# Attention's values' products one step later, with a fourth buffer, and a tile's transposes 12 steps later

## The chip, the cores and the metric

The kernel runs on one core of a Trainium2 chip. The metric is device time in microseconds (us) of one execution. The core's engines each work through a queue of their own in order: TensorE (PE) multiplies matrices, VectorE (DVE) and GpSimd (POOL) work elementwise, ScalarE (ACT) evaluates functions and casts, SyncE (SP) issues transfers. They wait for each other through semaphores.

## What is computed

The reference is one layer of a hybrid model on 2048 tokens of width 1024: retention with 4 heads in both directions, attention with 8 query heads and 2 key/value heads over 2048 own and 256 context keys, a projection, and a feed-forward part.

```python
ret = _ret_out(_bidir_retention(rq_h, rk_h, rv_h, log_gamma, s_f, s_b), rg, ret_gn_g)
s = einsum('bqkgd,bskd->bkgqs', q, k).astype(f32) * ATT_SCALE
p = softmax(s, axis=-1)
att = einsum('bkgqs,bskd->bqkgd', p, v)
x = x + g1 * (concatenate([ret, att], -1) @ w_out)
h2 = _modulate(_rmsnorm(x, norm2_g), sh2, sc2)
x = x + g2 * (square(relu(h2 @ w_ff1)) @ w_ff2)
out = _rmsnorm(x, final_norm_g)
```

## The kernel before

The program has three stages: input projections (to about 640 us), attention with retention and the output projection woven through it (to about 1650 us), and the feed-forward part, which is two blocks of matmuls in Strassen form. The change lies in the second stage.

That stage is written as a table of events. `on(k, phase, fn)` puts a call into step k; the steps are run in order, and within a step the phases in this order: begin, scores, piece, maximum, early, exp, cast, low, chain, pe, values, late, dma. Each engine's queue is what these calls issue, in that order. There is no planner behind it.

Attention goes over 32 groups (16 tiles of 128 queries, from the last to the first, times 2 key/value heads). A group takes NK = 18 steps, one block of 128 keys each, and the next group follows without a gap. For key block i, counted from the group's own start k:

- step k + i: PE multiplies the scores into a psum buffer `st` (two matmuls, lines 205 and 206; two buffers), and a row-minimum product `mp` for the next groups (line 168 or 172; two buffers), which DVE reduces a step later (line 181).
- step k + i + 1: ACT takes the exponential into half of `p32` (line 211; three buffers of two blocks).
- for each pair j of blocks, step k + 2j + 3: ACT casts the pair to 16 bits, `phi` (line 215).
- step k + 2j + 4: the remainder `plo` = p - phi, either both halves on POOL (line 222; pairs 0, 2, 4, 6 and 7) or one half on DVE in this step and one in the next (line 224).
- step k + 2j + 6: PE multiplies plo and phi with the values (lines 238 and 239, 16 matmuls) into the accumulators `o0` and `o1`. In the step after a group's last pair, ACT evacuates them.

The pool `pp`, with three buffers to a name, holds `p32`, `phi` and `plo`.

Retention and the output projection go over the tiles in the same steps, one tile in RF = 35 steps. Both use psum banks 0 and 1 (`psX`), of which there is one each. For a tile whose output step is k = R0 + 43 + 35 n: retention's output and attention's output are transposed through bank 1 at k - 11 and k - 6 (line 1540), the products with w_out fill 16 of the steps k to k + 19 in bank 0 (lines 1555 to 1557, three matmuls each), the row is squared on ACT, its root is taken, POOL multiplies x by it at k + 24 (`norm`, line 1582), and PE transposes the new rows in two groups of four (`transpose_x`, line 1587) through bank 1. A step behind each group DVE multiplies by the scale (`modulate`, line 1592) and POOL adds the shift (line 1597); another step later SP stores the result (line 1600). The next tile but one uses bank 1 too: retention's heads stand at k + 32 to k + 35, and ACT copies them out at k + 36.

x stays in one of four buffers named `xr` from its fetch at k - 2 until the last transpose. The product of modulate lies in a buffer `u`, of which there are two; the squares of the next tile write their unused output to the same two.

For four tiles (those of t = 11 to 8) POOL and ACT also form sums of pairs of new rows for the feed-forward part (`h_pair`, lines 71, 72 and 1649), in 13 steps spread over 28, which start behind the stores. When attention is done, at step `done`, the first weights and products of the feed-forward part begin (`prelude`).

The two functions that set the steps, and the two that hold the buffers, are these.

Of the kernel before, what the change touches and what calls it, by code (L numbers as in the profile page):

```python
# [13 lines left out]
F16 = mybir.dt.float16  # L14
# [8 lines left out]
P = 128  # L23
# [6 lines left out]
NK = NT + NC  # L30
# [25 lines left out]
def layer_kernel(ctx: ExitStack, tc: tile.TileContext, a: dict, out: bass.AP):  # L56
# [87 lines left out]
    class Group:  # L144
# [66 lines left out]
            nc.scalar.activation(self.p[kt // 2][:, kt % 2], self.s.pop(kt), AF.Exp, scale=HD**-0.5)  # L211

        def cast(self, j):
            hi = self.hi[j] = pp.tile([P, 2, 512], F16, name="phi", tag="phi")
            nc.scalar.activation(hi, self.p[j], AF.Copy)  # L215

        def low(self, j, i=None):
            if i in (None, 0):
                self.lo[j] = pp.tile([P, 2, 512], F16, name="plo", tag="plo")
            lo, p, hi = self.lo[j], self.p[j], self.hi[j]  # L220
            if i is None:
                nc.gpsimd.tensor_tensor(lo, p, hi, op=ALU.subtract)  # L222
            else:
                nc.vector.tensor_tensor(lo[:, i], p[:, i], hi[:, i], op=ALU.subtract)  # L224
# [35 lines left out]
    groups = [Group(n, *o) for n, o in enumerate(order)]  # L260


    with ExitStack() as st, tc.manual_schedule():
# [332 lines left out]
        def post(s, col, kind, i, x):  # L596
# [69 lines left out]
            elif col == C_AQ:  # L666
# [22 lines left out]

                do(s + 5, "turned", high)  # L690
                do(s + 5, "vec", low)
                do(s + 6, "store", lambda: nc.sync.dma_start(aq_d[i], x["z"]))
            else:
# [47 lines left out]

                do(s + 4, "hi", high)
                do(s + 5, "low", low)
                do(s + 6, "turn", turn_k)
                do(s + 7, "vec", lambda: nc.vector.tensor_copy(ks[:, :, row * P : (row + 1) * P], x["pt"][:, :2]))

        def value_parts(s):
# [50 lines left out]
            for i in range(3):  # L798
                do(s + 7 + i, "aux", scaled, i)
                do(s + 8 + i, "hi", high, i)  # L800
                do(s + 9 + i, "low", low, i)
# [274 lines left out]
        def slots(*what):  # L1076
            return [first[g, col] + n for g, col, ns in what for n in ns]

        two = (0, 0, 1, 1, 2, 2, 3, 3, 4, 4, 5, 5)
        at = slots((0, C_RQ, range(4)), (0, C_RV, two), (1, C_AQ, (1, 2, 3, 4)), (1, C_RK, (0, 0, 1, 2, 2, 3, 4, 4, 5)))  # L1080
# [6 lines left out]
        at = slots((0, C_AKV, range(1, 6)), (0, C_AQ, range(4)), (0, C_RQ, range(4)), (1, C_AQ, range(6)))  # L1087
# [12 lines left out]
        for i in range(NK):  # L1100
            at = min(s + i + 1, len(units) - 1)
# [128 lines left out]
    def pool(stack, name, bufs=1, **kw):  # L1230
        return stack.enter_context(tc.tile_pool(name=name, bufs=bufs, reuse_waits="tile", **kw))
# [4 lines left out]
    pp = pool(attn, "pp", 3)  # L1236
# [32 lines left out]
    def on(k, phase, fn, *args):  # L1269
        events.setdefault((k, phase), []).append((fn, args))  # L1270
# [25 lines left out]
    LAG = 22  # L1296
    ats = {}

    def attention():
        for n, g in enumerate(groups):  # L1300
            k = NK * n
            if n > 0:
                on(k - 14, "dma", g.load)
                on(k - 1, "late", g.minima, sm)
                for i in range(NK):
                    on(k + i, "piece", g.piece, i)
                    on(k + i + 1, "maximum", g.maximum, i)
            else:
                on(k + NK, "begin", g.load)
            on(k + NK, "chain", g.least, mts[n % 2])  # L1310
            on(k + NK + 1, "piece", g.turn)
            on(k + NK + 2, "cast", g.rows)
            on(k + NK + 3, "early", g.rows2)
            k += LAG
            for i in range(NK):
                on(k + i, "scores", g.scores, i)
                on(k + i + 1, "exp", g.exp, i)
            for j in range(NK // 2):
                on(k + 2 * j + 3, "cast", g.cast, j)
                if j in POOL_PAIRS:  # L1320
                    on(k + 2 * j + 4, "low", g.low, j)
                else:
                    for i in range(2):
                        on(k + 2 * j + 4 + i, "low", g.low, j, i)
                on(k + 2 * j + 6, "values", g.values, j)
            k += NK + 5
            on(k, "cast", g.evacuate)
            on(k + 1, "chain", g.invert)
            on(k + 2, "late", g.combine, ats)
        return NK * len(groups) + LAG + 8  # L1330

# [195 lines left out]
    def output_tile(t, k, last):  # L1529
# [94 lines left out]
                rest.extend([(f, q) for f in (transpose_x, modulate, shift_, store_h)])  # L1624
            return made, made + 5
        for q in range(2):
            at = k + (31 if t == 1 else 27) + q
            on(at, "pe", transpose_x, q)
            on(at + 1, "early", modulate, q)
            on(at + 1, "late", shift_, q)  # L1630
            on(at + 2, "dma", store_h, q)
# [39 lines left out]
    for i in range(3):  # L1671
        on(18 + i, "begin", more_keys, 0, i)
        on(26 + 4 * i, "late", more_keys, 1, i)
    done = attention()
    retention(24)
    output_weights(44)
    for n, t in enumerate(range(NT - 1, -1, -1)):
        made_at, last = output_tile(t, R0 + 43 + RF * n, n == NT - 1)
        if t in halves[0][4:]:
            for i, step in enumerate(h_pair(0, 11 - t)):  # L1680
                on(last + (2 + i if i < 2 else 4 + 2 * i), "dma" if i < 2 else "late", step)
# [424 lines left out]
    with tc.manual_schedule():  # L2106
# [8 lines left out]
        k = min(events)[0]  # L2115
# [67 lines left out]
```

## Time and profile before

| | us |
|---|---|
| median of 3 runs | 2825.27 (2821.01 to 2826.14) |
| profiled execution | 2820.49 |
| its span | 2818.7 |
| PE busy in the span | 2666.1 (95%) |
| DVE busy | 2180.7 (77%) |
| POOL busy | 1931.8 (69%) |
| ACT busy | 1467.6 (52%) |
| mean granted PE clock | 0.988 |

The profiled execution is the source of every duration below; it lies within the runs' spread. In the views, a row names the source line, the engine and the operation as out<-in, and a wait is written as "who <- for whom". [...] PEld is the loading of weights, which goes on beside the matmuls.

### The profile page before, as it was taken

How to read it: one execution, taken by the hardware profiler on the slowest of the kernel's cores; microseconds unless marked ns; L12 is line 12 of the kernel's file. 1: busy time of each engine (PE TensorE's matmuls, PEld its weight loads, DVE VectorE, ACT ScalarE, POOL GpSimd, SP SyncE). 2: the span in 40 equal slices, each digit the busy share in tenths (PEclk: the TensorE clock that was granted, in tenths of full speed). 3: DMA queues.
4: the chain of work that ended last, by engine and by line, in shares of the span. 5: the costliest groups of instructions: out<-in, count | busy, mean ns of one | idle time of the engine just before them, and what ended most of it. 6: DMA issues, size and time to landing. Idle time of an engine off the chain costs nothing.

```text
span 2818.7 us, 46098 instructions
## 1 busy us (share of the span) xinstructions
PE 2666.1 (95%) x16756; PEld 1600.5 (57%) x16756; DVE 2180.7 (77%) x3122; ACT 1467.6 (52%) x2443; POOL 1931.8 (69%) x1499
## 2 busy tenths in 40 slices
PE   6999999997899998999999889999999999999997
PEld 3878788875566665665666544444444444444443
DVE  3678748858987777787777469888876688888898
ACT  2534444425777777777777645555554322222232
POOL 2627428316865668787666679888775688888887
PEclk9999999999999999999999999999999999999998
DMA  6776956827312123333212454777783757575543
GB/s 213 271 258 212 325 216 204 270 100 236 114 43 75 52 66 101 117 93 95 63 61 73 172 163 132 230 249 244 244 275 106 254 180 283 173 275 172 188 142 112
DMA packets 330466, 482.81 MB, mean 171 GB/s; under 512 B 82807, under 2 KB 193655, under 8 KB 325758
## 3 DMA queue, kind: packets, MB, share of 16 engines
q1 hardware_dynamic: 329854, 479.60, 52.0%
q8 instruction: 132, 2.16, 0.3%
q14 instruction: 96, 0.79, 0.1%
q10 hardware_dynamic: 384, 0.26, 0.0%
HBM read 327.57 MB, written 152.20 MB: 170 GB/s over the span
## 4 chain that ended last, share of the span: by engine, by line
PE 57%; DVE 8%; POOL 5%; issue 3%; DMA 2%; ACT 1%; SPq 0%; POOLq 0%; DVEq 0%; ACTq 0%
PE pu L1789 7%; PE pu L1790 7%; PE pu L1791 7%; PE pd L2008 5%; PE pd L2007 5%; PE pd L2006 5%; PE o L239 3%; PE st L205 3%; PE st L206 3%; PE mp L168 2%; DVE nm L181 2%; PE bank L1555 2%; PE bank L1557 2%; PE bank L1556 2%; PE o L238 2%
## 5 line engine op out<-in xcount | busy, mean ns | idle before, releaser
L181 DVE TENSOR_REDUCE nm<-mp 128x1 f32<-128x512 f32 (+1 forms) x576 | 390.7, 684 | 172.3 <-PE mp L168 143.4
L222 POOL TENSOR_TENSOR plo<-p,phi 128x1024 f16<-128x1024 f32 x160 | 353.6, 2211 | 162.6 <-ACT phi L215 130.5
L211 ACT ACTIVATE p<-st 128x512 f32<-128x512 f32 x576 | 338.5, 598 | 197.7 <-PE st L206 122.4
L1789 PE MATMUL pu<-hf,w1f 128*128 128x512 f16 x896 | 340.9, 380 | 0.0
L2008 PE MATMUL pd<-w,uf 128*128 128x512 f16 x896 | 339.6, 379 | 1.3 <-DVE uf L1999 1.2
L1790 PE MATMUL pu<-hf,w1f 128*128 128x512 f16 x896 | 340.7, 380 | 0.0
L1791 PE MATMUL pu<-hf,w1f 128*128 128x512 f16 x896 | 340.6, 380 | 0.0
L2006 PE MATMUL pd<-w,uf 128*128 128x512 f16 x896 | 339.6, 379 | 0.0
L2007 PE MATMUL pd<-w,uf 128*128 128x512 f16 x896 | 339.6, 379 | 0.0
L215 ACT ACTIVATE phi<-p 128x1024 f16<-128x1024 f32 x288 | 303.9, 1055 | 0.0
L1020 PE MATMUL pso<-whi,hlo_l 128*128 128x512 f32 (+1 forms) x768 | 288.4, 376 | 10.6 <-DVE hlo_l L488 10.5
L1018 PE MATMUL pso<-whi,hhi_l 128*128 128x512 f32 (+1 forms) x768 | 296.9, 387 | 0.0
L1019 PE MATMUL pso<-wlo,hhi_l 128*128 128x512 f32 (+1 forms) x768 | 287.1, 374 | 1.7 <-DVE wlo L512 1.7
L238 PE MATMUL o<-wv,plo 128*128 128x65 f16 x2304 | 235.6, 193 | 25.2 <-POOL plo L222 18.1
L224 DVE TENSOR_TENSOR plo<-p,phi 128x512 f16<-128x512 f32 x256 | 240.9, 942 | 16.5 <-ACT phi L215 15.9
L2046 POOL TENSOR_TENSOR d<-d,g2b 128x512 f32<-128x512 f32 x126 | 200.9, 1595 | 69.5 <-DVE d L2018 67.7
L239 PE MATMUL o<-wv,phi 128*128 128x129 f16 x2304 | 243.4, 221 | 0.0
L238 PEld LDWEIGHTS <-plo 128*128 128x128 f16 x2304 | 206.3, 98 | 61.6 <-POOL plo L222 28.2
L1801 DVE TENSOR_TENSOR r<-pu,r 128x512 f32<-128x512 f32 x224 | 151.0, 686 | 111.2 <-PE pu L1791 92.2
L1806 POOL TENSOR_TENSOR r<-r 128x512 f32<-128x512 f32 x128 | 169.0, 1326 | 93.7 <-ACT r L1805 93.3
L205 PE MATMUL st<-qr,ks 128*128 128x512 f16 x576 | 219.6, 381 | 9.8 <-ACT p L211 9.7
L168 PE MATMUL mp<-ks,qr 128*128 128x512 f16 x512 | 196.3, 383 | 30.7 <-DVE nm L181 23.8
(324 smaller groups left out, 6306.3 us busy)
## 6 DMA issues: line engine op xcount, KB each, us to landing
wm<-in_w_ff SPq DMA_DIRECT2D x64, 512.0 KB, 6.7
u<-r SPq DMA_DIRECT2D x128, 256.0 KB, 4.8
ur<-u SPq DMA_DIRECT2D x128, 256.0 KB, 5.7
y<-x SPq DMA_DIRECT2D x64, 512.0 KB, 6.4
wst<-in_w_in SPq DMA_DIRECT2D x60, 512.0 KB, 6.6
wf<-w2f SPq DMA_DIRECT2D x112, 256.0 KB, 3.6
w<-wf SPq DMA_DIRECT2D x28, 1024.0 KB, 10.7
w1r<-in_w_ff SPq DMA_DIRECT2D x48, 512.0 KB, 5.7
```

Source lines behind the costliest of these rows:

```text
L181: nc.vector.tensor_reduce(dst, src, axis=AX.X, op=ALU.max, negate=True)
L205: mm(ps, ks[:, self.g, k], q[:, 0], start=True, stop=False)
L211: nc.scalar.activation(self.p[kt // 2][:, kt % 2], self.s.pop(kt), AF.Exp, scale=HD**-0.5)
L222: nc.gpsimd.tensor_tensor(lo, p, hi, op=ALU.subtract)
L238: mm(o[:, : HD + 1], lo[:, i, c], v[:, : HD + 1], start=False, stop=False)
L239: mm(o, hi[:, i, c], v[:, :VW], start=False, stop=last)
L1789: mm(pu[hf, i], whi, hi, start=k == 0, stop=False)
L1790: mm(pu[hf, i], whi, lo, start=False, stop=False)
L1791: mm(pu[hf, i], wlo, hi, start=False, stop=k == 3)
L2006: mm(ps, u[:, 0, b], w[:, b, 0], start=b == 0, stop=False)
L2007: mm(ps, u[:, 0, b], w[:, b, 1], start=False, stop=False)
L2008: mm(ps, u[:, 1, b], w[:, b, 0], start=False, stop=b == 3)
```

## The change

Four things are changed. The values' products of pair j are issued at k + 2j + 7, and a group's evacuation, its reciprocal and its combination also one step later; `attention` returns an end one step later, which moves the prelude. `phi` and `plo` have four buffers rather than three. The transposes of a tile's new rows stand at k + 39 and k + 41 rather than k + 27 and k + 28, with modulate, shift, store and, for the four tiles that have it, the pairs' work that follows. The tiles t = 1 (k + 31 and k + 32) and t = 0 (behind the loop) keep their places.

```diff
         def cast(self, j):
-            hi = self.hi[j] = pp.tile([P, 2, 512], F16, name="phi", tag="phi")
+            hi = self.hi[j] = pp.tile([P, 2, 512], F16, name="phi", tag="phi", bufs=4)
             nc.scalar.activation(hi, self.p[j], AF.Copy)

         def low(self, j, i=None):
             if i in (None, 0):
-                self.lo[j] = pp.tile([P, 2, 512], F16, name="plo", tag="plo")
+                self.lo[j] = pp.tile([P, 2, 512], F16, name="plo", tag="plo", bufs=4)
...
-                on(k + 2 * j + 6, "values", g.values, j)
-            k += NK + 5
+                on(k + 2 * j + 7, "values", g.values, j)
+            k += NK + 6
             on(k, "cast", g.evacuate)
             on(k + 1, "chain", g.invert)
             on(k + 2, "late", g.combine, ats)
-        return NK * len(groups) + LAG + 8
+        return NK * len(groups) + LAG + 9
...
         for q in range(2):
-            at = k + (31 if t == 1 else 27) + q
+            at = k + (31 + q if t == 1 else 39 + 2 * q)
             on(at, "pe", transpose_x, q)
             on(at + 1, "early", modulate, q)
             on(at + 1, "late", shift_, q)
             on(at + 2, "dma", store_h, q)
```

On PE, before, at the step in which retention's scores (L1394) of a tile begin, in the middle of the stage (st are scores, mp the row-minimum product, xr the normalized rows of the tile before, o the accumulators):

```order
L239 MATMUL o_11573<-wv,phi 128x129
L205 LDWEIGHTS ks
L205 MATMUL st<-qr,ks 128x512
L206 LDWEIGHTS ks_6522
L206 MATMUL st<-qr,ks_6522 128x512
L168 LDWEIGHTS qr
L168 MATMUL mp<-ks,qr 128x512
L1394 MATMUL bank_11926<-oqt,okt 128x128 x4
L1587 MATMUL bank_11931<-ident,xr 128x128 x4
L205 LDWEIGHTS ks
L205 MATMUL st<-qr,ks 128x512
```

On PE, after, at the same place:

```order
L205 LDWEIGHTS ks
L205 MATMUL st<-qr,ks 128x512
L206 LDWEIGHTS ks_6522
L206 MATMUL st<-qr,ks_6522 128x512
L168 LDWEIGHTS qr
L168 MATMUL mp<-ks,qr 128x512
L1394 MATMUL bank_11910<-oqt,okt 128x128 x4
L238 LDWEIGHTS plo
L238 MATMUL o_11588<-wv,plo 128x65
```

The values' products, which stood ahead of this step's scores, now stand behind the step's other work, and the transposes of xr are gone from here.

On PE, after, the place in the next tile to which the first of these transposes has come (mt are the row minima that are turned):

```order
L1557 MATMUL bank_12105<-wo,rl 128x512
L205 LDWEIGHTS ks
L205 MATMUL st<-qr,ks 128x512
L206 LDWEIGHTS ks_6522
L206 MATMUL st<-qr,ks_6522 128x512
L192 MATMUL mp<-ident,mt_6530 128x128 x4
L168 LDWEIGHTS qr
L168 MATMUL mp<-ks,qr 128x512
L1587 MATMUL bank_12216<-ident,xr 128x128 x4
L238 LDWEIGHTS plo
```

They stand among the next tile's output products (L1557 in the step before), again ahead of the values of their step.

On SP the stores of a tile's new rows (h<-u) stood together, after that tile's of load and ahead of the fetch of the next x. Now, for one tile (ogate is retention's gate, oqt, okt, ork and orv the next loads):

```order
L1356 DMA of<-sf_179 128x512
L1534 DMA xr<-in_x 128x1024
L157 DMA qr<-aq_128 64x4x128
L158 DMA qr<-aq_128 64x2x128
L157 DMA qr<-aq_128 64x4x128
L158 DMA qr<-aq_128 64x2x128
L1600 DMA h_201<-u 128x512
L1356 DMA ogate<-rg_114 128x512
L1600 DMA h_201<-u 128x512
L1356 DMA oqt<-qt_145 128x512
```

The two stores stand behind the next x and a group's four qr loads, with the gate's load between them.

## The prediction

> **What bounds the kernel now.** I read the page first: the engines' busy time, and the chain that ended last.
>
> ```profile
> span 2818.7 us, 46098 instructions
> PE 2666.1 (95%) x16756; PEld 1600.5 (57%) x16756; DVE 2180.7 (77%) x3122; ACT 1467.6 (52%) x2443; POOL 1931.8 (69%) x1499
> PE 57%; DVE 8%; POOL 5%; issue 3%; DMA 2%; ACT 1%; SPq 0%; POOLq 0%; DVEq 0%; ACTq 0%
> ```
>
> TensorE (PE) is busy for 95% of the span and leads the chain, so only time in which PE stands still can be won. The change touches the attention stage, so the table of windows comes next (us, busy time and instruction count of PE, PEld, DVE, ACT and POOL, then granted clock, DMA share, GB/s).
>
> ```profile
> 640.00:745.00 105.00, 87.18 (x842) 63.47 (x841) 96.32 (x188) 71.86 (x113) 79.45 (x55) 1.00 0.70 217
> 745.00:1060.00 315.00, 293.77 (x2757) 192.57 (x2755) 252.65 (x436) 240.82 (x393) 207.16 (x151) 0.99 0.19 56
> 1060.00:1300.00 240.00, 218.50 (x1990) 142.17 (x1988) 184.29 (x310) 182.36 (x304) 197.42 (x150) 0.98 0.38 106
> 1300.00:1610.00 310.00, 295.26 (x2740) 193.34 (x2738) 227.89 (x403) 230.87 (x380) 199.21 (x153) 1.00 0.26 86
> ```
>
> From 640 to 745 DVE is busy 96.32 of 105 us: that stretch is DVE's, and I count no gain in it. From 745 to 1610 PE is busy 807.5 of 865 us, so 57 us are idle. Who PE waits for there is the third view (total us, times, longest):
>
> ```profile
> PE o L238 <- POOL plo L222: 17.2, 14, 2.5
> PE mp L168 <- DVE nm L181: 9.4, 21, 1.4
> PE st L205 <- ACT p L211: 8.3, 12, 1.9
> PE bank L1587 <- POOL xr L1582: 6.7, 9, 1.5
> PE bank L1540 <- DVE u L1592: 5.2, 10, 1.3
> PE o L238 <- DVE plo L224: 5.1, 10, 1.0
> PE bank L1587 <- DVE u L1592: 0.5, 2, 0.4
> ```
>
> Line 238 is the values' product, lines 1587 and 1540 are transposes through the one psum bank 1. These five of the seven rows are what the change touches; the rows of mp and st are what it can make worse. The last view is the work of one step, as groups of this same window (busy us, mean ns):
>
> ```profile
> L205 PE MATMUL st<-qr,ks 128*128 128x512 f16 x515 | 196.0, 381 | 8.4 <-ACT p L211 8.3
> L211 ACT ACTIVATE p<-st 128x512 f32<-128x512 f32 x517 | 304.1, 598 | 169.0 <-PE st L206 107.1 <-POOL plo L222 35.1 <-DVE plo L224 20.6
> L215 ACT ACTIVATE phi<-p 128x1024 f16<-128x1024 f32 x259 | 273.3, 1055 | 0.0
> L222 POOL TENSOR_TENSOR plo<-p,phi 128x1024 f16<-128x1024 f32 x144 | 316.1, 2196 | 150.6 <-ACT phi L215 122.1 <-issue 16.2 <-DVE xr L1562 7.8
> ```
>
> 515 scores in 865 us make 1.68 us per step, 3.36 us per pair of steps. How the pieces lie in time is seen in one pair without output products in its second step (start, us, engine):
>
> ```profile
> 1086.50 0.60 ACT L211 ACTIVATE p<-st 128x512 f32<-128x512 f32 x1 [0.76 <-PE st L206]
> 1087.00 1.05 ACT L215 ACTIVATE phi<-p 128x1024 f16<-128x1024 f32 x1
> 1087.11 0.19 PE L238 MATMUL o<-wv,plo 128*128 128x65 f16 x1
> 1087.81 0.38 PE L205 MATMUL st<-qr,ks 128*128 128x512 f16 x1
> 1088.02 0.38 PE L206 MATMUL st<-qr,ks 128*128 128x512 f16 x1
> 1088.44 0.60 ACT L211 ACTIVATE p<-st 128x512 f32<-128x512 f32 x1 [0.39 <-PE st L206]
> 1088.93 0.87 ACT L1432 ACTIVATE oo<-oo,mr,cy_gn 128x128 f32<-128x128 f32 x2
> 1089.80 0.38 PE L205 MATMUL st<-qr,ks 128*128 128x512 f16 x1
> ```
>
> Three things are read here. A 512-column matmul is 0.38 us long, but the next starts 0.21 us behind it, so each row of idle time above hides some 0.16 us per stall. The values' products of one pair take 0.70 us of PE (1087.11 to 1087.81). And the casts (L215) stand between the exponentials of the even and of the odd step.
>
> **The change part by part, and its price.**
>
> *Values one step later.* No product is added. The products of a pair now stand behind the next step's scores and row-minimum product (three matmuls, 0.65 us) and whatever else PE has in that step; on average that is half of 3.36 less 0.70, or 1.33 us. So a wait on plo shrinks by 0.65 to 1.33 us; I take 1.0. POOL's 14 waits are 17.2/14 + 0.16 = 1.39 us each; some are shorter than 1.0, so I take 12 of their 19.4 us. DVE's ten are 5.1/10 + 0.16 = 0.67 us each and go whole: 6.7 us.
>
> *The fourth buffers.* L215, which fills phi, has 0.0 us idle before it, and POOL's L222 waits for phi's content (122.1 us), not for a place: buffers held nobody up, and the fourth is worth nothing by itself. It only keeps it so when a buffer is held a step longer. Bounds 0 and 1 us; I take 0.
>
> *Transposes 12 (and 13) steps later.* They wait for POOL's norm (L1582), whose result then lies 15 steps back, not 3; the bank is free after ocopy three steps ahead of them; the two groups stand two steps apart, so the second no longer follows on DVE's modulate, and neither do the transposes of L1540. Idle removed at most: 6.7 + 5.2 + 0.5 and 21 times 0.16, 15.8 us. But POOL is full where the largest of them lie:
>
> ```profile
> 1115.56 1.28 POOL L1388 TENSOR_TENSOR oqb<-oqt,tb 128x512 f32<-128x512 f32 x1
> 1116.80 1.16 POOL L72 TENSOR_TENSOR hp<-hs,hp 128x512 f16<-128x512 f32 x1
> 1117.95 1.12 POOL L1582 TENSOR_SCALAR xr<-xr,cy_f 128x1024 f32<-128x1024 f32 x1
> 1119.04 2.13 POOL L222 TENSOR_TENSOR plo<-p,phi 128x1024 f16<-128x1024 f32 x1
> 1122.57 2.48 POOL L1597 TENSOR_TENSOR u<-u,s 128x512 f32<-128x512 f32 x2
> 1119.12 0.66 PE L1587 MATMUL bank<-ident,xr 128*128 128x128 f32 x4 [1.05 <-POOL xr L1582]
> ```
>
> If L1587 no longer waits until 1119, the values that follow still wait for the plo that ends at 1121.17: PE merely gets there earlier. I take 60% of the 15.8, 9.5 us; the bounds are 5 (only the L1540 part) and 15.8.
>
> What else moves with them: modulate on DVE, shift (2.48 us for two) on POOL, two stores per tile on SP. The stores now stand behind the fetch of the next x and a group's four qr loads, and the gate's load behind the first of them. SP waits there for the shift; the gate is needed eight steps (13 us) later, so it is covered; without that cover each late load would cost POOL up to its landing time. The buffers of u are shared with the squares, whose next turn comes five steps (8 us) after the store is issued, against this landing time (last column, us):
>
> ```profile
> h<-u SPq DMA_DIRECT2D x32, 256.0 KB, 2.0
> ```
>
> Price 0, bounds 0 and 3 us. x stays 12 steps longer in its buffer, 43 of a 35-step period, so two of four buffers live: 0. The four tiles that also form h pairs do this 13 steps later, over the same lump of POOL work in the next tile: 0, bounds -4 and +4 us.
>
> *The clock.* Stalls in a row also cost clock:
>
> ```profile
> 1177.00:1180.30 3.30, 1.42 (x11) 0.99 (x10) 1.49 (x3) 0.34 (x1) 3.30 (x3) 1.00 0.71 141
> 1180.40:1187.00 6.60, 5.64 (x32) 3.98 (x33) 3.52 (x7) 3.21 (x5) 6.20 (x5) 0.50 0.27 76
> ```
>
> After a stretch with PE busy for 1.42 of 3.30 us, the clock is 0.50 for 6.6 us, which costs 3.3 us. I take 2.5 us back, bounds 0 and 5. [...]
>
> *What gets worse.* With the values moved, an odd step's scores follow the even step's 0.70 us sooner, while ACT is still in the cast. In the pair shown, the odd exponential would start when the cast ends, 1088.05, and end at 1088.65; the scores that need its buffer start at 1089.80 - 0.70 = 1089.10. The room falls from 0.76 to 0.45 us. ACT's other work between 745 and 1610 is 654.1 busy less 304.1 and 273.3, 76.7 us, about 118 lumps of 0.65 us; each that falls there overdraws 0.2 us. The output products, heads and scores of retention fill 21 of 35 steps and give room; in the other 40%, 47 lumps by 0.2 are 9.4 us. The minima (L168) lose the same 0.70 us against DVE: the room is wider, I take 2 us, bounds 0 and 5.
>
> *The end.* Everything after attention comes one step later, so one up-projection part (three matmuls) fewer stands ahead of this stall:
>
> ```profile
> 1619.87 0.66 PE L1587 MATMUL bank<-ident,xr 128*128 128x128 f32 x4 [4.45 <-POOL xr L1582]
> ```
>
> Its cover shrinks by 3 times 0.216: +0.65 us.
>
> Sum: -12 - 6.7 - 9.5 - 2.5 + 9.4 + 2 + 0.65 = -18.65 us. The profiled execution took 2820.49 us, 4.8 below the median of 2825.27; 2820.5 - 18.65 = 2801.8, and beside the median 2806.6. I forecast 2807 us.
>
> **Rivals.**
>
> *All of it comes out.* ACT's lumps fall where products give room, the transposes' waits do not return: -12 - 6.7 - 15.8 - 2.5 + 0.65 = -36 us, 2789 us. For it: outside 1060 to 1300 POOL is busy for only 207.16 of 315 us. Against it: the room of 0.45 us.
>
> *POOL keeps its lumps.* PE arrives earlier and waits for the same low parts: the 12 us of POOL's plo and 6.7 of the transposes' gain come back, -18.65 + 18.7 = 0, 2825 us. For it: between 1060 and 1300 POOL is busy 197.42 of 240 us. Against it: half of the waits lie elsewhere.
>
> *Slower: ACT becomes late for the odd scores.* ACT's exponential waits 35.1 + 20.6 = 55.7 us, in 39 stalls of 1.43 us, until a low part frees a p32 buffer, of which three are left as they are. With 0.45 us of room each such stall could reach PE as 0.98 us: 39 x 0.98 = 38 us, -18.65 + 38 = +19, 2844 us. It decides once exponentials end later than 0.45 us after where the shown pair has them, in most pairs. Against it: PE paid only 8.3 us on st so far.
>
> **How the numbers follow.** The sum's own case, 2796 to 2818 by its terms' bounds: 0.52. All comes out: 0.20. POOL keeps its lumps: 0.12. ACT late: 0.16. A difference under 0.2% (5.6 us) cannot be told from none in this kernel. Faster is 0.52 + 0.20 = 0.72, the same 0.12, slower 0.16. The range 2780 to 2830 holds the first three and the mild part of the last.
>
> **What the profile after would show.** Waits of L238 on plo at some 8 us rather than 22; L1587 and L1540 waits on xr and u nearly gone between 745 and 1610; L205 on ACT's p risen from 8 to some 17 us; fewer windows at half clock. I am wrong if the rows of st or mp grow by more than those of plo and the transposes shrink.

## The result, and the profile after

The changed kernel took 2824.40 us (median of 12 runs, 2821.59 to 2829.39), the kernel before 2822.74 us in the same comparison: a ratio of 1.0009, 95% interval 1.0002 to 1.0016. So nothing was won; by the interval 0.6 to 4.5 us were lost. Forecast were 2807 us. The profiled execution of before, 2820.49 us, lies below the three runs that were given with it (from 2821.01 us) and within the twelve of this comparison (2817.19 to 2826.49 us).

The page of the changed kernel's profiled execution:

```profile
span 2822.9 us, 46094 instructions
PE 2664.2 (94%) x16756; PEld 1604.0 (57%) x16756; DVE 2193.4 (78%) x3122; ACT 1457.6 (52%) x2443; POOL 1928.3 (68%) x1499
```

Who PE waits for between 745 and 1610 us, after (the view that the prediction shows of before):

```profile
PE st L205 <- ACT p L211: 16.4, 23, 2.5
PE mp L168 <- DVE nm L181: 15.1, 27, 1.8
PE o L238 <- POOL plo L222: 10.8, 8, 2.3
PE mp L192 <- DVE mt L187: 6.6, 6, 1.7
PE mp L172 <- DVE nm L181: 3.5, 6, 1.1
```

The transposes' rows (L1587, and L1540 on u) are gone, the values' wait on DVE is gone, that on POOL is down from 17.2 to 10.8 us. St is up from 8.3 to 16.4, and what ends in mp (L168, L172, and L192, the turning of the minima) is up from 11.9 to 25.2 us. For plo, the transposes and st that is near the forecast; for mp it is not. But this window does not cut the two programs at the same places: of the first five groups it holds 51.9 us before and 62.4 us after. From the first scores of the sixth group to the last scores of all, PE's waits are these. Before:

```profile
PE o L238 <- POOL plo L222: 16.9, 13, 2.5
PE bank L1587 <- POOL xr L1582: 6.7, 9, 1.5
PE mp L168 <- DVE nm L181: 6.1, 16, 1.0
PE bank L1540 <- DVE u L1592: 5.2, 10, 1.3
PE o L238 <- DVE plo L224: 4.3, 9, 1.0
PE st L205 <- ACT p L211: 2.7, 7, 0.6
PE mp L192 <- DVE mt L187: 1.2, 2, 0.7
...
```

After:

```profile
PE o L238 <- POOL plo L222: 10.8, 8, 2.3
PE mp L168 <- DVE nm L181: 10.2, 20, 1.2
PE st L205 <- ACT p L211: 7.3, 17, 0.9
PE mp L192 <- DVE mt L187: 6.6, 6, 1.7
PE mp L172 <- DVE nm L181: 2.2, 4, 1.1
```

Waits on plo fall by 10.4 us, and those of the transposes are gone (12.4 us, with a row of 0.5 that is not shown). St rises by 4.6 us, and mp by 11.2, from 7.8 (L172 has 0.5 of it) to 19.0. So there is a gain in this stretch. It is lost at both its ends, which is seen when the stage is cut at the same places of the program: first scores, first scores of the sixth group, last scores, first transposes of tile t = 1. Before:

```profile
638.50:796.90 158.40, 129.83 (x1233) 91.62 (x1232) 144.62 (x260) 112.28 (x178) 120.33 (x79) 0.98 0.51 157
796.90:1589.30 792.40, 746.53 (x6954) 488.95 (x6953) 606.40 (x1058) 602.82 (x989) 549.64 (x414) 0.99 0.26 76
1589.30:1619.90 30.60, 24.15 (x166) 13.45 (x162) 14.40 (x25) 13.11 (x25) 15.18 (x17) 1.00 0.89 346
```

After:

```profile
643.60:807.40 163.80, 131.27 (x1231) 93.51 (x1232) 147.81 (x259) 111.33 (x178) 117.96 (x79) 0.96 0.49 152
807.40:1583.90 776.50, 737.90 (x6935) 486.92 (x6932) 616.53 (x1056) 593.41 (x988) 547.42 (x412) 1.00 0.27 78
1583.90:1623.60 39.70, 25.20 (x182) 14.72 (x181) 16.27 (x27) 13.82 (x26) 18.11 (x19) 0.89 0.64 245
```

The first five groups take 5.4 us more, the stretch behind them 15.9 us less, the tail 9.1 us more: -1.4 us in all. From there to the end of the span it is 1198.8 and 1199.4 us. The 5.1 us by which the first scores start later (643.6 against 638.5) come from ahead of any changed instruction; they are this execution's, and the medians differ by 1.7 us only.

### The profile page after: what moved, and what is told of

Read it like the earlier page. It is cut to its first block, busy times and chain, and to the rows that moved or that the text cites. A ratio compares the mean times of both kernels' runs of the same rounds, so it can differ in the third digit from the quotient of the medians.

```text
span 2822.9 us, 46094 instructions
## 1 busy us (share of the span) xinstructions
PE 2664.2 (94%) x16756; PEld 1604.0 (57%) x16756; DVE 2193.4 (78%) x3122; ACT 1457.6 (52%) x2443; POOL 1928.3 (68%) x1499
## 3 DMA queue, kind: packets, MB, share of 16 engines
q1 hardware_dynamic: 329854, 479.60, 51.9%
## 4 chain that ended last, share of the span: by engine, by line
PE 57%; DVE 9%; POOL 3%; issue 2%; DMA 2%; ACT 2%; SPq 0%; POOLq 0%; DVEq 0%; ACTq 0%
PE pu L1789 7%; PE pu L1790 7%; PE pu L1791 7%; PE pd L2006 5%; PE pd L2007 5%; PE pd L2008 5%; PE o L239 3%; DVE plo L224 3%; PE st L205 3%; PE st L206 3%; PE mp L168 3%; DVE nm L181 2%; PE bank L1555 2%; PE bank L1557 2%; PE bank L1556 2%
## 5 line engine op out<-in xcount | busy, mean ns | idle before, releaser
L224 DVE TENSOR_TENSOR plo<-p,phi 128x512 f16<-128x512 f32 x256 | 256.4, 1003 | 18.5 <-ACT phi L215 13.4
L238 PE MATMUL o<-wv,plo 128*128 128x65 f16 x2304 | 232.9, 193 | 10.8 <-POOL plo L222 10.8
L168 PE MATMUL mp<-ks,qr 128*128 128x512 f16 x512 | 196.6, 384 | 35.8 <-DVE nm L181 28.5
```

The source lines that it names most:

```text
L238: mm(o[:, : HD + 1], lo[:, i, c], v[:, : HD + 1], start=False, stop=False)
```

## The experiments

Measured first, so that the verdicts can be read against it. "First five", "rest" and "tail" are the first three stretches above, from one profiled execution each; a ratio is to the kernel before on the same chip, with its 95% interval.

| kernel | median us | ratio | first five | rest | tail |
|---|---|---|---|---|---|
| before | 2822.2 to 2822.7 | 1 | 158.4 | 792.4 | 30.6 |
| changed | 2824.40 | 1.0009 (1.0002 to 1.0016) | 163.8 | 776.4 | 39.7 |
| values alone | 2825.19 | 1.0011 (1.0002 to 1.0020) | 164.4 | 789.3 | 30.1 |
| transposes alone | 2822.21 | 0.9998 (0.9989 to 1.0007) | 157.3 | 784.5 | 38.0 |
| all but tile 2 | 2816.09 | 0.9981 (0.9972 to 0.9991) | 165.5 | 779.1 | 30.2 |
| tile 2 alone | 2832.05 | 1.0027 (1.0017 to 1.0037) | 160.4 | 792.4 | 38.3 |
| values two later | 2816.75 | 0.9974 (0.9965 to 0.9984) | 159.5 | 780.4 | 32.4 |
| three buffers | 2821.09 | 0.9991 (0.9980 to 1.0001) | 165.2 | 776.9 | 39.7 |
| four p32 | 2819.20 | 0.9987 (0.9975 to 0.9998) | 163.2 | 783.6 | 30.5 |
| values from group 6 | 2812.84 | 0.9962 (0.9948 to 0.9977) | 158.7 | 781.6 | 30.4 |
| two later, four p32 | 2811.76 | 0.9965 (0.9952 to 0.9978) | 161.5 | 776.3 | 31.2 |
| transposes but tile 2 | 2817.48 | 0.9978 (0.9967 to 0.9989) | 161.0 | 789.3 | 29.7 |
| POOL's low later | 2810.11 | 0.9960 (0.9947 to 0.9974) | 160.3 | 778.7 | 30.7 |
| DVE's low later | 2817.63 | 0.9983 (0.9973 to 0.9992) | 163.5 | 781.4 | 30.7 |

Kernels that have the same program up to the sixth group (before, tile 2 alone, values from group 6, and the two with transposes alone) differ by up to 3.7 us in "first five": that is the spread of one execution. In "rest" the two kernels with transposes alone, which differ in tile 2's only, are 4.8 us apart, so differences of a few us there are not safe either.

### Which part, and which place

Values alone, against the kernel before:

```diff
-tag="phi")
+tag="phi", bufs=4)
-tag="plo")
+tag="plo", bufs=4)
-on(k + 2 * j + 6, "values", g.values, j)
-k += NK + 5
+on(k + 2 * j + 7, "values", g.values, j)
+k += NK + 6
-return NK * len(groups) + LAG + 8
+return NK * len(groups) + LAG + 9
```

> The values' products one step later with the four buffers; the transposes stay where they stood before. Measure for the tail: from the last scores to the first transposes of tile t = 1, 30.6 us before and 39.7 us in the changed kernel. Theory A (the tail's loss comes from tile t = 2's second store, behind which SP's seven loads of hf now stand): the tail is within 2 us of 30.6, attention keeps about half of its gain of 10 us, 2818 us against 2823. Rival B (the tail's loss comes from the prelude, one step later): the tail is 39 us here too, 2827 us. Rival C (the values' later place gives nothing, since st and mp wait for as much as plo no longer does): tail 30.6, attention as before, 2823 us.

Transposes alone:

```diff
-at = k + (31 if t == 1 else 27) + q
+at = k + (31 + q if t == 1 else 39 + 2 * q)
```

> The transposes 12 and 13 steps later; values, buffers and prelude as before. Theory A: the tail is 39 us, attention gains 6 to 9 us by the transposes alone, about 2823 us. Rival B: the tail is 30.6 us and the time 2815 us. Rival C: attention gains all its 10 us here, and with A's tail 2821 us.

The whole change without tile t = 2's transposes, against the changed kernel:

```diff
-at = k + (31 + q if t == 1 else 39 + 2 * q)
+at = k + ({1: 31, 2: 27}[t] + q if t in (1, 2) else 39 + 2 * q)
```

> The whole change, but tile t = 2's transposes stay at k + 27 and k + 28. Theory A: the loads of hf are issued some 8 us sooner than in the changed kernel, the tail is back at about 31 us, 2816 us, 8 under the changed kernel. Rival B: the tail stays at 39 us, 2824 us, as the changed kernel.

Tile t = 2 alone, against the kernel before:

```diff
-at = k + (31 if t == 1 else 27) + q
+at = k + (39 + 2 * q if t == 2 else (31 if t == 1 else 27) + q)
```

> The kernel before with one edit: tile t = 2's transposes at k + 39 and k + 41. Theory A: nothing but the tail changes, which becomes 38 to 40 us; 2831 us, 8 over before. Rival B: 2823 us, as before.

Three of the four came out as theory A has it, to within 1.1 us. The tail's loss follows the place of tile 2's transposes and not the prelude's: 38.0 and 38.3 us with them moved and the prelude at its old step, 30.1 and 30.2 us with the prelude a step later and them at their old place. Undoing this one place is worth 8 us (2816.09 against 2824.40), doing it alone costs 9 (2832.05; 5 to 10 by the ratio's interval).

How it costs them is seen on SP's queue. Before:

```profile
1585.53 1.77 SPq L1600 DMA_DIRECT2D h<-u  x2
...
1589.72 11.13 SPq L1779 DMA_DIRECT2D hf<-hf  x7
...
1608.36 1.49 SPq L1572 DMA_DIRECT2D x<-xr  x1
```

After:

```profile
1593.52 0.34 SPq L1600 DMA_DIRECT2D h<-u  x1
...
1597.04 0.32 SPq L1600 DMA_DIRECT2D h<-u  x1
1597.45 3.73 SPq L1779 DMA_DIRECT2D hf<-hf  x7
...
1605.32 8.76 SPq L1572 DMA_DIRECT2D x<-xr  x1
```

The seven loads of hf, 1 MB each, and the weights behind them keep the transfers busy in the tail (a DMA share of 0.89 and 346 GB/s in before's row of it). After, they stand behind tile 2's second store, and SP waits there for POOL's shift of those rows, which ends at 1597.01, until 1597.04. The loads that were issued from 1589.72 on, while attention still ran, are issued from 1597.45 on, although attention ends 5 us sooner. Tile 1's x is stored behind them (it lands 10.1 us after its issue before, 16.8 after), and POOL's norm, which overwrites x, waits for that store, 8.47 and 14.04 us. POOL's norm of tile 1, before and after:

```profile
1618.69 1.12 POOL L1582 TENSOR_SCALAR xr<-xr,cy_f 128x1024 f32<-128x1024 f32 x1 [8.47 <-DMA x<-xr]
```

```profile
1622.41 1.12 POOL L1582 TENSOR_SCALAR xr<-xr,cy_f 128x1024 f32<-128x1024 f32 x1 [14.04 <-DMA x<-xr]
```

and without tile 2's move:

```profile
1614.42 1.12 POOL L1582 TENSOR_SCALAR xr<-xr,cy_f 128x1024 f32<-128x1024 f32 x1 [7.03 <-DMA x<-xr]
```

Counted from the last scores, the norm starts after 29.4, 38.5 and 29.0 us. Tile 1's transposes wait for it, and PE with them: for 4.45 us before (the row that the prediction shows for the end), and after:

```profile
1623.58 1.12 PE L1587 MATMUL bank<-ident,xr 128*128 128x128 f32 x4 [12.25 <-POOL xr L1582]
```

Values alone is the miss: 2825.19 us where 2818 were expected. The tail is as A has it, but the first five groups lose 6 us, and the rest gains 3.1. There the plo waits did go, and others took their place:

```profile
PE st L205 <- ACT p L211: 14.9, 17, 2.5
PE bank L1587 <- POOL xr L1582: 14.3, 10, 3.1
PE mp L168 <- DVE nm L181: 13.8, 23, 1.8
...
PE o L238 <- POOL plo L222: 3.2, 1, 3.2
```

PE, no longer stopped by plo, reaches the transposes sooner and waits there for POOL's norm, 14.3 us rather than 6.7. With the transposes alone it is the other way round:

```profile
PE o L238 <- POOL plo L222: 24.5, 22, 3.0
PE mp L168 <- DVE nm L181: 13.1, 20, 2.0
PE st L205 <- ACT p L211: 6.5, 11, 1.5
```

plo's wait grew from 17.2 to 24.5 us. Each half hands part of its gain to the other's wait, since both end on POOL; together they win 16 us in the rest, singly 3.1 and 7.9. The waits show it more firmly than these three differences of single executions do.

### One step, two steps, and buffers

Values two steps later, tile 2 as before, against the changed kernel:

```diff
-on(k + 2 * j + 7, "values", g.values, j)
-k += NK + 6
+on(k + 2 * j + 8, "values", g.values, j)
+k += NK + 7
-return NK * len(groups) + LAG + 9
+return NK * len(groups) + LAG + 10
-at = k + (31 + q if t == 1 else 39 + 2 * q)
+at = k + ({1: 31, 2: 27}[t] + q if t in (1, 2) else 39 + 2 * q)
```

> As the run that keeps tile t = 2's transposes (2816.1 us), but the values two steps later than before, so that they stand in even steps again, with all the room that a step of either kind gives. Theory D (one step is harmful by its parity: the odd scores follow too soon on ACT and DVE): the first five groups take 158 us again rather than 165, PE waits for st 8 us and for plo under 3 us between 745 and 1610, 2806 us. Rival E (it is the lateness of the values itself, not the parity): the first five groups stay at 164 us, PE waits for st stay at 14 us, and only the plo waits fall: 2812 us.

The first five groups are back (159.5 us), so their loss belongs to the odd step, not to lateness. But st did not fall to 8 us. It rose:

```profile
PE st L205 <- ACT p L211: 31.2, 27, 3.5
```

while ACT waits for low parts to free p32:

```profile
ACT p L211 <- DVE plo L224: 38.1, 18, 4.6
ACT p L211 <- POOL plo L222: 22.5, 15, 3.7
```

When the values no longer stop PE for a late low part, the scores do, one buffer further on. Both theories named only a part of it: 2816.75 us, where they had 2806 and 2812.

Three buffers for phi and plo, against the changed kernel: the two `bufs=4` are taken out.

> The changed kernel with three buffers for phi and plo, as before the change. If the fourth buffer is worth nothing, 2824 us, within 2 us of the changed kernel. If buffers held one step longer hold up casts or low parts, PE waits for plo and st grow and the time is above 2830 us.

2821.09 us, 3.3 under the changed kernel, where 2 at most were expected; the ratios' intervals (0.9980 to 1.0001, and 1.0002 to 1.0016) just miss each other. So the fourth buffers win nothing here. Why the kernel without them should be 3 us below the changed one stays open: its profiled execution, itself one of 2825.44 us, shows nearly the same three stretches.

The fourth buffer for p32 (phi and plo three, tile 2 as before), against the changed kernel:

```diff
-name="p32", tag="p32")
+name="p32", tag="p32", bufs=4)
-tag="phi", bufs=4)
+tag="phi")
-tag="plo", bufs=4)
+tag="plo")
-at = k + (31 + q if t == 1 else 39 + 2 * q)
+at = k + ({1: 31, 2: 27}[t] + q if t in (1, 2) else 39 + 2 * q)
```

> As the run that keeps tile t = 2's transposes (2816.1 us), but the fourth buffer goes to p32, and phi and plo have three. Theory F (the scores' waits come from exponentials that wait for a low part to free p32): ACT's waits on plo fall from 56 us to under 20, PE's wait for st from 14.6 to about 6 us, 2808 us. Rival (they come from the cast that stands ahead of the odd exponential): PE's wait for st stays at 12 to 15 us, 2816 us.

ACT's waits for low parts nearly vanish (POOL's are 3.4 us, DVE's are not among the longest), but st only falls to 10.8 us and mp and plo rise:

```profile
PE mp L168 <- DVE nm L181: 19.2, 30, 1.8
PE o L238 <- POOL plo L222: 11.8, 7, 3.2
PE st L205 <- ACT p L211: 10.8, 10, 2.5
```

The time (2819.20 us) does not fall: with the values one step later p32's buffers are not what binds. Both, two steps and four p32 buffers, against the kernel before:

```diff
-name="p32", tag="p32")
+name="p32", tag="p32", bufs=4)
-on(k + 2 * j + 6, "values", g.values, j)
-k += NK + 5
+on(k + 2 * j + 8, "values", g.values, j)
+k += NK + 7
-return NK * len(groups) + LAG + 8
+return NK * len(groups) + LAG + 10
-at = k + (31 if t == 1 else 27) + q
+at = k + ({1: 31, 2: 27}[t] + q if t in (1, 2) else 39 + 2 * q)
```

> Values two steps later, four buffers for p32, three for phi and plo, the transposes 12 and 13 steps later but for tile t = 2. With the values out of the way PE waited 31 us for st, behind exponentials that waited for p32. If p32's buffers are what bound there: PE's wait for st falls to some 12 us, the stretch from the sixth group to the last scores is 770 us rather than 780, 2807 us. If DVE and POOL bound it, whatever holds their results: the waits move to mp, the stretch stays at 780 us, 2815 us.

2811.76 us, between the two; st is down to 13.5 us as the first has it, the stretch only to 776.3, since mp is at 17.7 us.

The transposes without tile 2 and nothing else:

```diff
-at = k + (31 if t == 1 else 27) + q
+at = k + ({1: 31, 2: 27}[t] + q if t in (1, 2) else 39 + 2 * q)
```

> The kernel before with the transposes 12 and 13 steps later, but for tile t = 2; values and buffers as before. From the run with all transposes (2822.2 us) less the 8 us of the tail: 2814 us, the first five groups 158, the stretch behind them 785, the tail 30.5 us. If the transposes' gain needs the values' later place: above 2819 us.

2817.48 us, 5 below before; its profiled execution (2823.04 us) is a late one of its runs, which may be why its first two stretches stand above what was expected. Beside 2816.09 us it says that the values' move as made adds nothing measurable to the transposes'.

### The first five groups

Values at their old place in the first five groups, one step later from the sixth on, tile 2 as before, against the changed kernel:

```diff
-on(k + 2 * j + 7, "values", g.values, j)
-k += NK + 6
+on(k + 2 * j + 6 + (n >= 5), "values", g.values, j)
+k += NK + 5 + (n >= 5)
-at = k + (31 + q if t == 1 else 39 + 2 * q)
+at = k + ({1: 31, 2: 27}[t] + q if t in (1, 2) else 39 + 2 * q)
```

> As the run that keeps tile t = 2's transposes (2816.1 us), but the first five groups keep the values where they stood before, and only the groups from the sixth on have them one step later. If the 5 to 7 us that the first five groups lose come from the values' place there: they take 158 us again, 2810 us. If they come from elsewhere (the clock, the loads of that run): 164 us, 2816 us.

158.7 us, and 2812.84 us, nearer to the 2810 expected than to the 2816: the loss belongs to the values' place in these groups. The five kernels that only move the values one step there ("changed", "values alone", "all but tile 2", "three buffers", "four p32") take 163.2 to 165.5 us for them, the seven with the values at even steps 157.3 to 161.5.

How the place costs it is less plain. DVE is busy for 144.6 of 158.4 us before, and for 147.8 of 163.8 after. What has grown most are DVE's 38 low parts, here before and after, each over its first stretch (busy us, mean ns):

```profile
L224 DVE TENSOR_TENSOR plo<-p,phi 128x512 f16<-128x512 f32 x38 | 42.5, 1119 | 0.8 <-ACT phi L215 0.8
```

```profile
L224 DVE TENSOR_TENSOR plo<-p,phi 128x512 f16<-128x512 f32 x38 | 48.1, 1266 | 0.0
```

The same instruction takes 0.67 to 0.69 us where nothing of POOL's runs beside it (87 of them in the trace after). After, in the first group, POOL and DVE:

```profile
655.08 2.13 POOL L222 TENSOR_TENSOR plo<-p,phi 128x1024 f16<-128x1024 f32 x1 [1.46 <-ACT phi L215]
```

```profile
655.21 2.55 DVE L224 TENSOR_TENSOR plo<-p,phi 128x512 f16<-128x512 f32 x1
```

DVE's low part starts 0.13 us behind POOL's and ends 0.55 us behind its end. That looks as if it had stood still while POOL ran; this is my reading, the rows show the times alone. In this trace, of the 148 of DVE's 256 low parts that start while an instruction of POOL runs, 125 end 0.50 to 0.61 us behind that one's end, and 13 end before it. Two runs move one of the two against the other, in the first five groups only, both against the run with all but tile 2 (1 line each):

```diff
-on(k + 2 * j + 4, "low", g.low, j)
+on(k + 2 * j + 4 + (n < 5), "low", g.low, j)
```

> As the run that keeps tile t = 2's transposes (2816.1 us; first five groups 165.5 us, in which DVE's 38 low parts take about 50 us), but in the first five groups POOL's low parts are issued one step later, so they meet DVE's low parts in another way. Theory G (the first five groups are longer because DVE's low parts are held up while POOL's run): the 38 low parts and the stretch change together, by about the same us; if the low parts fall to 43 us, the stretch falls to 159 us and the time to 2810 us. Rival (clock or scores): the low parts change and the stretch stays at 163 to 166 us.

```diff
-on(k + 2 * j + 4 + i, "low", g.low, j, i)
+on(k + 2 * j + 4 + i + (n < 5), "low", g.low, j, i)
```

> As the same run, but in the first five groups DVE's low parts are issued one step later and POOL's stay. Theory G: again the stretch moves by what the 38 low parts move, in either direction. Rival: the stretch stays at 163 to 166 us, or it grows because exponentials wait longer for p32, with the low parts unchanged.

The low parts, with POOL's later:

```profile
L224 DVE TENSOR_TENSOR plo<-p,phi 128x512 f16<-128x512 f32 x38 | 42.0, 1105 | 0.0
```

with DVE's later:

```profile
L224 DVE TENSOR_TENSOR plo<-p,phi 128x512 f16<-128x512 f32 x38 | 45.4, 1195 | 0.0
```

Against 49.8 us in the run they start from, the low parts fall by 7.8 and 4.4 us, the stretch (165.5 us) by 5.2 and 2.0; the 2.0 lie within the spread of one execution. With POOL's low parts a step later the time is 2810.11 us, the best of the study, and 0.40% under before (0.26 to 0.53%). With DVE's it is 2817.63 us, no better than the 2816.09 of the run they start from.

The first of the two looks like theory G, but DVE is not less busy by it. The stretch in the run they start from, and with POOL's low parts later:

```profile
640.90:806.30 165.40, 132.97 (x1232) 94.08 (x1231) 150.20 (x260) 111.38 (x178) 117.70 (x79) 0.95 0.47 150
```

```profile
643.70:804.00 160.30, 131.74 (x1231) 93.22 (x1232) 149.37 (x259) 111.69 (x178) 120.72 (x78) 0.97 0.49 155
```

DVE's busy time, the third in the row, is 150.20 and 149.37 us. Other subtractions of two SBUF tiles on DVE, those that split w_out, have become longer instead, in the same order:

```profile
L1514 DVE TENSOR_TENSOR wo<-wos,wo 128x512 f16<-128x512 f32 x16 | 16.0, 1001 | 4.2 <-ACT wo L1512 4.2
```

```profile
L1514 DVE TENSOR_TENSOR wo<-wos,wo 128x512 f16<-128x512 f32 x16 | 22.6, 1415 | 0.2
```

What fell is DVE's idle time, from 15.2 to 10.9 us, and the clock rose from 0.95 to 0.97. The clock record of the traces, which the column averages, has half clock for 6.0 us of this stretch before, 11.9 after, 17.6 in the run they start from and 10.0 with POOL's low parts later. At half clock matmuls of 512 columns follow each other by 0.43 us (before, at 1184.77 and 1185.20), at full clock by 0.21 (at 1187.73 and 1187.94). So by my estimate a us at half clock costs at most half a us, and up to 3.8 of the 5.2 us may be clock. The clock is not all of the loss: tile 2 alone has nearly the changed kernel's time at half clock (11.7 us), but low parts of 44.9 rather than 48.1 us and a stretch of 160.4 rather than 163.8 us. Nor are the low parts: two later with four p32 has 37.6 us of them and a stretch of 161.5 us. So it is shown that the values' odd step costs these groups 5 to 6 us, and that DVE's low parts grow with it (47.4 to 50.1 us in the five kernels named above, 37.6 to 44.9 in the seven); how the loss divides between low parts, clock and other waits stays open.

## Why the prediction was wrong

The forecast was 18.65 us faster by a sum of seven terms, of which all but one were read in the window from 745 us on. The two steps that failed lie at the stage's two ends, and one term between them was mis-sized. Term by term, with the waits of the stretch from the sixth group's first scores to the last scores:

- *Values later, -18.7, and transposes later, -9.5, with 60% coming out.* Right, taken together. The waits on plo and of the transposes fell by 10.4 and 12.4 us; with the 0.16 us that the prediction adds for each of the 14 and 21 stalls gone, that is 28.4 us against 28.2. The plo waits that were to return for the transposes' are there when these move alone (17.2 to 24.5 us between 745 and 1610). Alone, the values are worth little, 3.1 us in the rest, though plo's waits nearly vanish (22.3 to 3.2 us between 745 and 1610): PE meets POOL's lag at the next thing that POOL owes.
- *Odd scores behind the cast, +9.4.* Right in kind, two thirds of the size: st from 2.7 to 7.3 us, +4.6, or 6.2 with 0.16 for each of ten more stalls. Between 745 and 1610 it is +8.1, but 3.5 of that are the first five groups', of which more lie in that window after. The rival that multiplied this did not happen.
- *Minima against DVE, +2, at most 5.* Mis-sized: 7.8 to 19.0 us, +11.2, or 12.8 with ten more stalls. L192, which turns a group's minima through the same buffers, had been left out of the sum; it went from 1.2 to 6.6 us. And not all comes from the values' place: with the transposes alone it is 11.7 us, and 13.0 without tile 2's.
- *Clock, -2.5.* Not tested apart. In these two executions half clock falls from 10.2 to 3.4 us of the stretch, which by the same estimate is worth 3.4 us; but tile 2 alone, with before's program there up to that tile's transposes, has 6.8.
- *Fourth buffers, 0.* They win nothing, by the run with three; that this run is 3 us faster is not explained.
- *The stores on SP, 0, at most 3, and +0.65 for the end.* This is the first of the two steps that failed. I had weighed the gate's load and the buffers of u behind the stores, for a tile in the middle, and not what stands behind the stores of tile 2 at the stage's end: seven loads of hf. It cost 8 to 9 us, shown in both directions. The end's own +0.65, for the prelude a step later, did not show (tail 30.1 and 30.2 against 30.6 us).
- *First five groups, "DVE's, and I count no gain in it".* The second. A stretch in which another engine is the bound was priced at zero for gains, and so for losses too. It lost 5 to 6 us by the values' odd step. DVE's low parts grow there (42.5 to 48.1 us), and so does the time at half clock (6.0 to 11.9 us); the shares are open. The stretch also reaches to 797 us and not to 745, so its last 52 us were priced as if PE were the bound there.

So, by the stretches above: forecast for the rest was -19.3 us (all terms but the end), measured -16, of which some 2 us are matmuls that now come behind the last scores (one pair's values, and tile 2's transposes). The terms as measured, -28.4 + 6.2 + 12.8 - 3.4, with these 2 us make -14.8, so they account for nearly all of it. The two ends were forecast at +0.65 and measured at +14.5. The prediction's own sign of being wrong, that st or mp grow by more than plo and the transposes shrink, did not come (15.8 against 22.8 us in this stretch): it looked where the forecast was nearly right. The rival "POOL keeps its lumps" had the right time, 2825 us, by chance and not by its reason: PE's waits for POOL did shrink. I gave 0.12 to no change. The case of the sum was given as 2796 to 2818 us "by its terms' bounds"; the upper bounds of the terms (buffers, transposes, stores, pairs, clock, minima) add 18 us to 2807, which is 2825.

## What to carry to other kernels

When a store is moved in its queue, look at every place where it comes to stand, first and last iterations above all, and ask what is queued behind it there: here the prefetches of the next stage were the dearest (issued from 1597.45 rather than 1589.72 on, the tail 39.7 rather than 30.6 us). A stretch that another engine bounds isn't worth zero: moving work there can change which instructions run beside each other, and how long they take changed with it here (DVE's 38 low parts 48.1 rather than 42.5 us). Compare two profiles between the same places of the program, not between the same times. Two waits on the same late engine are one wait; price their removal together (here 3.1 and 7.9 us singly, 16 together).

## What the runs showed of the hardware that I had not expected

DVE's subtraction of two SBUF tiles takes 0.67 to 0.69 us where nothing of POOL's runs beside it and 2.55 us in the pair above, where POOL's low part does, and the extra time is shown as DVE's own busy time. So a DVE that is busy for 92% (96.32 of 105 us before) may be so in part with such extra time: at 0.68 us each, the 38 low parts of the first five groups would by my estimate be 26 us, where 42.5 were measured. In the pair of rows above DVE's ends 0.55 us behind POOL's end; by what means the one holds up the other, if it does, no run here shows.
